# A two-layer trunk on one core: gate and up as 7 quarter products, down products between them, banded pooling

## Chip, core, metric

The kernel runs on one core of a Trainium2 chip. The metric is the device time of one execution in microseconds; the median of three runs before the change is 1806.95.

## What is computed

Tokens x (512 x 1024) pass two layers. Each layer has a SwiGLU feed-forward network (FFN) ahead of its mixer and one behind it, so there are four FFNs, each with its own weights and a root-mean-square norm of its input:

```python
def swiglu(u, wg, wu, wd):
    return (jax.nn.silu(u @ wg) * (u @ wu)) @ wd
...
h = h + 0.5 * swiglu(rmsnorm(h, ffn_pre_norm[l]), ffn_pre_wg[l], ffn_pre_wu[l], ffn_pre_wd[l])
u = rmsnorm(h, mix_norm[l])
```

wg and wu are 1024 x 2816, wd is 2816 x 1024. The mixer of the first layer is pooling: in four groups of 256 channels a causal mean over the last 2, 4, 8 or 16 tokens, less the token itself, times a 256 x 256 matrix. After the first layer the shared keys and values (kv) are made; the mixer of the second layer is latent attention over them. A final norm ends the program. All of it is float32.

## The kernel before

The residual lies transposed on the chip, as 8 tiles h0 to h7 of 128 channels x 512 tokens. Every product of float32 matrices is made as three products of rounded parts: each operand is split into a high part (ScalarE rounds it to fp32r) and a low part (VectorE subtracts), and `mm3` (L83 to L87) adds high x high, high x low and low x high in PSUM. `load_w` (L101) fetches 1024 columns of weights (512 KB) into one of four raw buffers, ScalarE casts them (L117), VectorE subtracts (L118).

`ffn` (L276) works on two halves of 11 blocks of 128 hidden features. For a block, 8 chunks x 3 matmuls of 512 tokens make gate, and as many make up. `gated` (L280) takes them out of PSUM: gate and up times the norm's factor (VectorE, L284 and L286), Silu (ScalarE), their product (GpSimd, L287), and the split of the product (ScalarE L290, VectorE L291). After 11 blocks come the 8 down products of that half, 33 matmuls each, added to h by VectorE (L324).

`Norm` (L209) follows each new h chunk: it multiplies by the gain and splits (`hi`, `lo`; L219, L224), squares it on ScalarE (L237) and adds the squares on GpSimd (L241). When all 8 chunks are there, TensorE sums over channels (L156), VectorE finds the reciprocal root with 12 small operations (`rsqrt`, L162), `on_all` (L193) builds a diagonal, multiplies it by ones on TensorE (L204) and ScalarE copies the result out (L206). The gate and up products use the unscaled h times the gain, so they don't wait for the norm's factor; only `gated` does.

In the pooling stage the products with the pooling matrices come first, and VectorE and GpSimd make the moving sums on 128 x 512 tiles by shifted additions (`shift`, L367 to L373); TensorE meanwhile runs products of the first blocks of the second FFN. At the very end the last two down products run in two halves of 256 tokens, and `first_half` (L719) norms and stores the first while the second is made. Before the fourth FFN stands the attention's output projection (`out_proj`, L531).

The order on each engine is that of a scheduler, except in the pooling stage, whose order on TensorE, VectorE and GpSimd is that of the code.

## Time and profile before

| what | us |
|---|---|
| three runs | 1803.35, 1806.95, 1807.29 |
| profiled execution: time, span of the records | 1802.47, 1800.7 |
| first FFN | 6.2 to 371.3 |
| pooling stage | 371.3 to 446.8 |
| second FFN | 446.8 to 773 |
| shared kv | 773 to 825 |
| third FFN | 825 to 1160 |
| attention | 1160 to 1428 |
| fourth FFN | 1428 to 1784.2 |
| last norm and store | to 1800.7 |

An execution's time is a little more than the span of its profile's records. The stages overlap by a few products; the limits are those of TensorE's work. Busy times count an engine's own instructions, and a matmul's duration in the records overlaps with the next one's: the pace is read from the distance of two starts.

### The profile page before, as it was taken

What the parts mean: (1) busy time and instruction counts of PE and PEld (TensorE: products, weight loads), DVE (VectorE), ACT (ScalarE), POOL (GpSimd) and SP (SyncE); (2) the same over time, 40 slices, a digit from 0 to 9 for tenths busy, and PEclk for the clock granted to TensorE, in tenths of its full rate; (3) what the DMA queues carried; (4) which work ended last, traced back from release to release, by engine and by line L of the source; (5) the groups of instructions that cost most, each with busy time, mean ns of one, the idle gap of its engine ahead of it and who ended that gap; (6) DMA issues with size and microseconds to landing.
All of it is one profiled execution on the core that took longest, in us unless ns stands there. A gap on an engine that the chain in (4) does not pass through costs nothing.

```text
span 1800.7 us, 20652 instructions
## 1 busy us (share of the span) xinstructions
PE 1757.8 (98%) x8120; PEld 1457.7 (81%) x8120; DVE 869.3 (48%) x1266; ACT 624.0 (35%) x940; POOL 340.0 (19%) x218
## 2 busy tenths in 40 slices
PE   8999999988999999999999999999999999999997
PEld 6888888866888888878888888888888888888886
DVE  7443444478443444456433443487665754334432
ACT  6322232323331233333322233277564432222221
POOL 3220022134220122102210122212121222101212
PEclk9999999989999999999999999999999999999998
DMA  7223223212222232223222322121231322322301
GB/s 258 94 94 103 96 94 96 104 59 70 92 96 94 96 103 94 94 87 107 94 94 99 100 94 76 59 71 51 74 94 59 129 94 96 103 94 94 101 29 47
DMA packets 49552, 165.77 MB, mean 92 GB/s; under 512 B 6448, under 2 KB 6448, under 8 KB 49456
## 3 DMA queue, kind: packets, MB, share of 16 engines
q1 hardware_dynamic: 49456, 164.46, 27.7%
q8 instruction: 64, 1.05, 0.2%
q14 instruction: 32, 0.26, 0.0%
HBM read 157.88 MB, written 2.10 MB: 89 GB/s over the span
## 4 chain that ended last, share of the span: by engine, by line
PE 93%; DVE 4%; issue 1%; ACT 1%; DMA 1%; SPq 0%; DVEq 0%; ACTq 0%
PE mm L85 30%; PE mm L86 29%; PE mm L87 29%; DVE s L372 1%; DVE wlo L118 1%; PE mm L615 1%; PE aux L156 1%; PE mm L614 1%; PE aux L651 1%; PE mm L626 0%; PE mm L616 0%; PE mm L627 0%; DVE gh_lo L224 0%; PE mm L651 0%; DVE h L381 0%
## 5 line engine op out<-in xcount | busy, mean ns | idle before, releaser
L85 PE MATMUL mm<-gh_hi,whi 128*128 128x512 f32 x1440 | 561.8, 393 | 15.8 <-ACT whi L117 6.2
L86 PE MATMUL mm<-gh_lo,whi 128*128 128x512 f32 x1440 | 565.0, 392 | 7.3 <-DVE gh_lo L224 7.3
L87 PE MATMUL mm<-gh_hi,wlo 128*128 128x512 f32 x1440 | 563.2, 392 | 0.0
L117 ACT CAST whi<-wraw 128x1024 fp32r<-128x1024 f32 (+2 forms) x332 | 315.2, 959 | 714.1 <-PE mm L86 647.1
L118 DVE TENSOR_TENSOR wlo<-wraw,whi 128x1024 fp32r<-128x1024 f32 (+2 forms) x302 | 372.4, 1235 | 195.6 <-ACT whi L117 195.1
L287 POOL TENSOR_TENSOR tu<-tu,tg 128x512 f32<-128x512 f32 x88 | 191.8, 2180 | 1014.7 <-ACT whi L117 762.7
L85 PEld LDWEIGHTS mm<-gh_hi,whi 128*128 128x128 f32 x1440 | 272.0, 189 | 76.3 <-ACT gh_hi L219 6.9
L86 PEld LDWEIGHTS mm<-gh_lo,whi 128*128 128x128 f32 x1440 | 272.6, 189 | 66.9 <-DVE gh_lo L224 9.8
L87 PEld LDWEIGHTS mm<-gh_hi,wlo 128*128 128x128 f32 x1440 | 272.5, 189 | 57.2 <-issue 0.2
L85 PE MATMUL mm<-mh,whi 128*128 128x512 f32 (+1 forms) x726 | 277.9, 383 | 0.0
L86 PE MATMUL mm<-ml,whi 128*128 128x512 f32 (+1 forms) x726 | 276.5, 383 | 0.0
L87 PE MATMUL mm<-mh,wlo 128*128 128x512 f32 (+1 forms) x726 | 276.4, 383 | 0.0
L286 DVE TENSOR_TENSOR tu<-mm,rb 128x512 f32<-128x512 f32 x88 | 60.8, 691 | 255.4 <-PE mm L87 255.4
L86 PEld LDWEIGHTS mm<-ml,whi 128*128 128x128 f32 x726 | 136.4, 188 | 26.7
L87 PEld LDWEIGHTS mm<-mh,wlo 128*128 128x128 f32 x726 | 136.4, 188 | 26.6
L85 PEld LDWEIGHTS mm<-mh,whi 128*128 128x128 f32 x726 | 136.4, 188 | 26.6
L291 DVE TENSOR_TENSOR ml<-tu,mh 128x512 fp32r<-128x512 f32 x88 | 62.7, 713 | 131.2 <-ACT mh L290 131.0
L290 ACT CAST mh<-tu 128x512 fp32r<-128x512 f32 x88 | 54.5, 621 | 188.0 <-POOL tu L287 187.2
L324 DVE SCALAR_TENSOR_TENSOR h<-mm,h 128x512 f32<-128x512 f32 (+1 forms) x66 | 44.5, 675 | 143.1 <-PE mm L87 143.0
L284 DVE TENSOR_TENSOR tg<-mm,rb 128x512 f32<-128x512 f32 x88 | 60.8, 691 | 80.7 <-PE mm L87 79.7
L241 POOL TENSOR_TENSOR sq_acc<-sq_acc,sq 128x512 f32<-128x512 f32 (+1 forms) x43 | 58.1, 1350 | 204.8 <-ACT sq L237 204.7
L118 POOL TENSOR_TENSOR wlo<-wraw,whi 128x512 fp32r<-128x512 f32 (+1 forms) x30 | 40.9, 1362 | 197.6 <-ACT whi L117 191.5
(158 smaller groups left out, 1424.8 us busy)
## 6 DMA issues: line engine op xcount, KB each, us to landing
wraw<-in_wgu SPq DMA_DIRECT2D x160, 512.0 KB, 3.3
wraw<-in_wd SPq DMA_DIRECT2D x88, 512.0 KB, 3.2
wraw<-in_wo SPq DMA_DIRECT2D x16, 512.0 KB, 3.3
wraw<-in_wfirst SPq DMA_DIRECT2D x12, 512.0 KB, 3.2
wraw<-in_wheads SPq DMA_DIRECT2D x8, 512.0 KB, 3.3
h<-in_xT SPq DMA_DIRECT2D x8, 256.0 KB, 5.6
wraw<-in_wfirst SPq DMA_DIRECT2D x8, 256.0 KB, 5.7
qr<-yh SPq DMA_DIRECT2D x32, 64.0 KB, 2.0
```

What stands on the lines that cost most here:

```text
L85: nc.tensor.matmul(out, w[0], x[0], start=start, stop=False)
L86: nc.tensor.matmul(out, w[0], x[1], start=False, stop=False)
L87: nc.tensor.matmul(out, w[1], x[0], start=False, stop=stop)
L117: nc.scalar.copy(hi[:, s], raw[:, s])
L118: lo_engines[i % len(lo_engines)].tensor_tensor(out=lo[:, s], in0=raw[:, s], in1=f(hi[:, s]), op=ALU.subtract)
L241: nc.gpsimd.tensor_tensor(out=self.acc[:, ts], in0=self.acc[:, ts], in1=self.sq[:, ts], op=ALU.add)
L284: nc.vector.tensor_tensor(out=tg, in0=gate, in1=rb, op=ALU.mult)
L286: nc.vector.tensor_tensor(out=tu, in0=up, in1=rb, op=ALU.mult)
L287: nc.gpsimd.tensor_tensor(out=tu, in0=tu, in1=tg, op=ALU.mult)
L290: nc.scalar.copy(hi, tu)
L291: nc.vector.tensor_tensor(out=lo, in0=tu, in1=f(hi), op=ALU.subtract)
L324: nc.vector.scalar_tensor_tensor(out=h[d][:, ts], in0=o[:, ts], scalar=0.5, in1=h[d][:, ts], op0=ALU.mult, op1=ALU.add)
```

## The change

Gate and up of one block g are x wg and x wu. Taken as one product of a matrix of quarters (channels 0 to 511 and 512 to 1023; the two outputs and the two token halves), they are made with 7 products instead of 8, by a form of Strassen's algorithm with 15 additions. Each product has 4 chunks of 128 channels x 3 matmuls x 256 tokens.

- Of the weights of a block, two 512 KB loads as before, four parts are split: gate's two quarters (`a`), one of up (`a22`), and the sums s1, s3 and s2, s4, whose four additions of 128 x 512 run on GpSimd (`group_weights`, L166). Before, the two loads alone were split. The raw buffers stay four, and the sums are made in place.
- Of h, `PairNorm` makes seven quarter operands per chunk pair (c, c + 4) in place of two halves: `row1` and `row2`, per pair 3 multiplications and 4 casts on ScalarE and 8 operations on VectorE.
- The outputs are put together by VectorE in PSUM and in small tiles (`p2`, `p7`, `p3`), in 7 operations of 256 tokens and one of 512 in place of two of 512; the product of gate and up moves from GpSimd to VectorE.
- The 22 blocks are in five parts (4, 4, 4, 4, 6). The down products of a part, two in each block, are laid behind the products of the next part's blocks, in PSUM tiles of another pool. Those of the last six blocks stand at the end. The order on TensorE is that of the code.
- Pooling: the pooling matrices' products are made with tokens on partitions, and the moving mean less the token is a product with a banded matrix of 128 x 144 (`pooled`), 9 matmuls a chunk. The shifted sums of VectorE and GpSimd, one to four a chunk, go.

```diff
+    def group_weights(raws, wb):
+        ra, rb = raws
+        q0, q1, whole = slice(0, 512), slice(512, UNIT), slice(0, UNIT)
+        def add(out, x, y):
+            nc.gpsimd.tensor_tensor(out=out, in0=x, in1=y, op=ALU.add)
+        a = split_w(ra, wsplit_sb, "w")
+        split_into(a, ra, whole)
+        a22 = split_w(rb[:, q0], room.wf, "f")
+        split_into(a22, rb[:, q0], q0)
+        add(rb[:, q0], rb[:, q0], rb[:, q1])
+        add(rb[:, q1], rb[:, q1], ra[:, q0])
+        s13 = split_w(rb, wsplit_sb, "w")
+        split_into(s13, rb, whole)
+        add(ra[:, q0], rb[:, q0], ra[:, q0])
+        add(ra[:, q1], ra[:, q0], ra[:, q1])
+        s24 = split_w(ra, wb, "w")
+        split_into(s24, ra, whole)
...
+        def row1(self, k):
+            b = self.b[k] = room.act.tile([P, 3, HT], F32, tag="g", name="b0", bufs=3)
+            nc.scalar.mul(b[:, ::2], h[k].rearrange("p (a b) -> p a b", a=2), gain(self.base, k))
+            nc.vector.tensor_tensor(out=b[:, 1], in0=b[:, 2], in1=b[:, 0], op=ALU.subtract)
+            ga = self.pair(resid, f"gh{k}")
+            self.split_pair(ga, b[:, :2].rearrange("p a b -> p (a b)"))
+            self.gh[k] = ga
+        def row2(self, k):
+            b = self.b.pop(k)
+            t1, b12 = b[:, 1], b[:, 2]
+            u = room.act.tile([P, 3, HT], F32, tag="g", name="b1", bufs=3)
+            c = k + ND // 2
+            b21, n22 = u[:, 0], u[:, 1]
+            nc.scalar.mul(b21, h[c][:, :HT], gain(self.base, c))
+            nc.scalar.mul(n22, h[c][:, HT:], g_neg[:, self.base + c:self.base + c + 1])
+            gb = self.pair(room.gx, f"gb{k}")
+            self.split_pair(gb, u[:, :2].rearrange("p a b -> p (a b)"))
+            t = room.act.tile([P, T], F32, tag="m", name="t24")
+            nc.vector.tensor_tensor(out=t[:, :HT], in0=t1, in1=n22, op=ALU.add)
+            nc.vector.scalar_tensor_tensor(
+                out=t[:, HT:], in0=t[:, :HT], scalar=-1.0, in1=b21, op0=ALU.mult, op1=ALU.subtract)
+            gc = self.pair(resid, f"gh{c}")
+            self.split_pair(gc, t)
+            t3 = room.act.tile([P, HT], F32, tag="c1", name="t3")
+            nc.vector.scalar_tensor_tensor(
+                out=t3, in0=n22, scalar=-1.0, in1=b12, op0=ALU.mult, op1=ALU.subtract)
+            if k % 2 == 0:
+                self.gd[k // 2] = self.pair(room.gx, f"gd{k // 2}")
+            self.split_pair(self.gd[k // 2], t3, slice(k % 2 * HT, (k % 2 + 1) * HT))
+            self.gh[c] = gb, gc
...
+            def product(g, to, w, x, ks=range(4), start=True, stop=True):
+                if start and ks[0] == 0:
+                    acc[g][to] = mm_tile()[:, :HT]
+                for k in ks:
+                    mm3(acc[g][to], weights[g][w](k), norm.operand(x, k), start and k == 0, stop and k == 3,
+                        skip_group_check=True)
...
+            def p1(g, ks=range(4)):
+                product(g, "x", "a11", "b11", ks)
+                if ks[-1] == 3:
+                    copy_of(g, "c1")
+            def p2(g, ks=range(4)):
+                product(g, "y2", "a12", "b21", ks)
+                if ks[-1] == 3:
+                    act[g]["g"] = room.act.tile([P, 3, HT], F32, tag="g", name="gate", bufs=3)
+                    y = acc[g]["y2"]
+                    nc.vector.tensor_tensor(out=y, in0=act[g].pop("c1"), in1=y, op=ALU.add)
+            def scaled(g, i, y):
+                nc.vector.tensor_tensor(
+                    out=act[g]["g"][:, i], in0=y, in1=factor["r"][:, i * HT:(i + 1) * HT], op=ALU.mult)
+            def p6(g):
+                product(g, "x", "s2", "n2", start=False)
+                copy_of(g, "c16")
+            def p5(g, ks=range(4)):
+                product(g, "y1", "s1", "t1", ks)
+            def p7(g):
+                product(g, "x", "s3", "t3", start=False)
+                t = copy_of(g, "c167")
+                nc.vector.tensor_tensor(out=t, in0=t, in1=acc[g]["y1"], op=ALU.subtract)
+            def p4(g):
+                product(g, "x", "a22", "t4", start=False)
+            def p3(g):
+                product(g, "y1", "s4", "n22", start=False)
+                y = acc[g].pop("y1")
+                nc.vector.tensor_tensor(out=y, in0=act[g]["c16"], in1=y, op=ALU.subtract)
+                scaled(g, 1, y)
+                gate = act[g]["g"][:, :2].rearrange("p a b -> p (a b)")
+                nc.scalar.activation(gate, gate, AF.Silu)
+                nc.vector.tensor_tensor(out=gate, in0=gate, in1=factor["r"], op=ALU.mult)
+                m = room.act.tile([P, T], F32, tag="m", name="m")
+                nc.vector.tensor_tensor(out=m[:, :HT], in0=acc[g].pop("x"), in1=gate[:, :HT], op=ALU.mult)
+                nc.vector.tensor_tensor(out=m[:, HT:], in0=act[g]["c167"], in1=gate[:, HT:], op=ALU.mult)
+                j = g % N_MID
                 hi = midp.tile([P, T], F32R, tag=f"mh{j}", name=f"mh{j}")
                 lo = midp.tile([P, T], F32R, tag=f"ml{j}", name=f"ml{j}")
...
+                nc.scalar.copy(hi, m)
+                nc.vector.tensor_tensor(out=lo, in0=m, in1=f(hi), op=ALU.subtract)
+                mids[g] = hi, lo
...
+            base, due, before = 0, [], None
+            for n in PARTS:
+                groups = list(range(base, base + n))
+                if base == 0:
+                    pair, groups = groups[:2], groups[2:]
+                    for g in pair:
+                        prepare(g)
+                    for k in range(3):
+                        for p in (p1, p5, p2):
+                            for g in pair:
+                                p(g, [k])
+                    for p in (p1, p5):
+                        for g in pair:
+                            p(g, [3])
+                    r = norm.r()
+                    for g in pair:
+                        p2(g, [3])
+                    p6(0)
+                    factor["r"] = norm.spread(r)
+                    for g in pair:
+                        scaled(g, 0, acc[g].pop("y2"))
+                    p6(1)
+                    p7(0)
+                    p7(1)
+                    p4(0)
+                    p3(0)
+                    before = 1
+                for g in groups:
+                    prepare(g)
+                    p1(g)
+                    p2(g)
+                    scaled(g, 0, acc[g].pop("y2"))
+                    p4(before)
+                    p6(g)
+                    p5(g)
+                    if g == NF - 1:
+                        p7(g)
+                        p3(before)
+                        p4(g)
+                        p3(g)
+                    else:
+                        p3(before)
+                        p7(g)
+                    before = g
+                    now, due = due[:2], due[2:]
+                    if len(due) == ND - 2:
+                        down_two(now, tile_of=aux_tile)
+                    else:
+                        for d in now:
+                            down(last_part, d, tile_of=aux_tile)
+                last_part, due = (base, n), list(ORDER)
+                base += n
...
+        def pooled(c):
+            g, cs, o = c // 2, slice(c * P, (c + 1) * P), mm_tile()
+            for tb in range(NQB):
+                n, table = min(BAND, T - tb * P), thi[:, g, int(tb == 0)]
+                os = o[:, tb * P:tb * P + n]
+                nc.tensor.matmul(os, vh[:, tb, cs], table[:, :n], start=tb == 0, stop=False, skip_group_check=True)
+                nc.tensor.matmul(os, vl[:, tb, cs], table[:, :n], start=False, stop=tb == NQB - 1,
+                                 skip_group_check=True)
+                if tb == 0:
+                    nc.tensor.matmul(o[:, :PAD], vh[:, tb, cs], tlo[:, g], start=False, stop=False,
+                                     skip_group_check=True)
             nc.vector.scalar_tensor_tensor(
...
+                out=h[c], in0=o, scalar=gain(G_PSCALE, c), in1=h[c], op0=ALU.mult, op1=ALU.add)
+            nxt.add(c)
+        with tc.manual_schedule(engines={mybir.EngineType.PE}):
+            os = {(0, tb): product(0, tb) for tb in range(NQB)}
             r = rms(norm.squares, D)
...
+            for tb in range(2):
+                os[1, tb] = product(1, tb)
+            for tb in range(NQB):
+                values_of(0, tb, os[0, tb])
+            for tb in range(2, NQB):
+                os[1, tb] = product(1, tb)
+            for tb in range(NQB):
+                values_of(1, tb, os[1, tb])
+            for c in ORDER:
```

**VectorE, start of the first FFN.** Before (gh_lo and wlo are the low parts of the x chunk and of the weights):

```order
L224 SCALAR_TENSOR_TENSOR gh0_lo_162<-h0_82,g_sb_90,gh0_hi_161 128x512
L118 TENSOR_TENSOR wlo_100<-wraw_98,whi_99 128x512
L224 SCALAR_TENSOR_TENSOR gh1_lo_168<-h1_83,g_sb_90,gh1_hi_167 128x512
L118 TENSOR_TENSOR wlo_100<-wraw_98,whi_99 128x512
L224 SCALAR_TENSOR_TENSOR gh2_lo_175<-h2_84,g_sb_90,gh2_hi_174 128x512
L118 TENSOR_TENSOR wlo_111<-wraw_109,whi_110 128x512
```

Each x chunk (of h_82, h_83, h_84) was followed by the piece of weights that goes with it. With the change (gb, gd, gh are low parts of x quarters with 0 to 3 the chunk, wraw_107 and wraw_109 the second loads of blocks 0 and 1, wraw_106 and wraw_108 the first):

```order
L354 TENSOR_TENSOR gb2_lo_218<-b1_214,gb2_hi_217 128x512
L354 TENSOR_TENSOR gd1_lo_231<-t3_228,gd1_hi_230 128x256
L375 TENSOR_TENSOR t24_256<-b0_237,b1_249 128x256
L381 SCALAR_TENSOR_TENSOR t3_263<-b1_249,b0_237 128x256
L354 TENSOR_TENSOR gh6_lo_225<-t24_221,gh6_hi_224 128x512
L354 TENSOR_TENSOR gh3_lo_241<-b0_237,gh3_hi_240 128x512
L376 SCALAR_TENSOR_TENSOR t24_256<-t24_256,b1_249 128x256
L157 TENSOR_TENSOR wlo_293<-wraw_106,whi_292 128x1024
L354 TENSOR_TENSOR gb3_lo_253<-b1_249,gb3_hi_252 128x512
L157 TENSOR_TENSOR wlo_307<-wraw_109,whi_306 128x1024
L354 TENSOR_TENSOR gd1_lo_231<-t3_263,gd1_hi_230 128x256
L354 TENSOR_TENSOR gh7_lo_260<-t24_256,gh7_hi_259 128x512
```

Now the operands of chunks 2 and 3 stand ahead of the last weight sums of both blocks.

**TensorE, start of the first FFN**, with the change, from the second item on (mm_320 and mm_328 are sums of block 1, whi_306 and wlo_307 its s1 and s3):

```order
L91 MATMUL mm_320<-gh0_hi_144,whi_296 128x256
L92 MATMUL mm_320<-gh0_lo_145,whi_296 128x256
L93 MATMUL mm_320<-gh0_hi_144,wlo_297 128x256
L91 MATMUL mm_324<-gh0_hi_144,whi_286 128x256
L92 MATMUL mm_324<-gh0_lo_145,whi_286 128x256
L93 MATMUL mm_324<-gh0_hi_144,wlo_287 128x256
L91 MATMUL mm_328<-gh0_hi_144,whi_306 128x256
L92 MATMUL mm_328<-gh0_lo_145,whi_306 128x256
L93 MATMUL mm_328<-gh0_hi_144,wlo_307 128x256
L91 MATMUL mm_332<-gb0_hi_153,whi_276 128x256
L92 MATMUL mm_332<-gb0_lo_154,whi_276 128x256
```

Before, four sums took one chunk after the other, high parts first. Now p1, p5 and p2 of both blocks take chunk 0, and p5 of block 1 comes fourth.

**TensorE, the last down products.** Before, inside the second token half (mm_13205):

```order
L86 MATMUL mm_13205<-ml8_12632,whi_13092 128x256
L87 MATMUL mm_13205<-mh8_12631,wlo_13093 128x256
L156 MATMUL aux_13163<-ones_157,sq_13159 128x1
L156 MATMUL aux_13163<-ones_157,sq_acc_12826 128x1
L156 MATMUL aux_13163<-ones_157,sq_13159 128x1
L85 MATMUL mm_13205<-mh9_12703,whi_13092 128x256
L86 MATMUL mm_13205<-ml9_12704,whi_13092 128x256
L87 MATMUL mm_13205<-mh9_12703,wlo_13093 128x256
L85 MATMUL mm_13205<-mh10_12775,whi_13092 128x256
L86 MATMUL mm_13205<-ml10_12776,whi_13092 128x256
```

The product that spreads the norm (L204) came after all of them. With the change, between the first token half (mm_18979) and the second (mm_19045):

```order
L91 MATMUL mm_18979<-mh5_18765,whi_18962 128x256
L92 MATMUL mm_18979<-ml5_18766,whi_18962 128x256
L93 MATMUL mm_18979<-mh5_18765,wlo_18963 128x256
L236 MATMUL aux_19003<-ones_138,sq_acc_18817 128x1
L236 MATMUL aux_19003<-ones_138,sq_18999 128x1
L236 MATMUL aux_19003<-ones_138,sq_acc_18817 128x1
L236 MATMUL aux_19003<-ones_138,sq_18999 128x1
L284 MATMUL aux_19025<-diag_19023,ones_138 128x256
L91 MATMUL mm_19045<-mh0_18085,whi_18925 128x256
L92 MATMUL mm_19045<-ml0_18086,whi_18925 128x256
L93 MATMUL mm_19045<-mh0_18085,wlo_18926 128x256
```

The token sums of the first half and the product that spreads its norm now stand together ahead of them.

## Rows read from the trace of the kernel before

**Rows 1.** The page, part 1: busy time, share of the span and instructions of each engine.

```profile
PE 1757.8 (98%) x8120; PEld 1457.7 (81%) x8120; DVE 869.3 (48%) x1266; ACT 624.0 (35%) x940; POOL 340.0 (19%) x218
```

**Rows 2.** Windows by stage: length, busy (x instructions) of PE, PEld, DVE, ACT, POOL; PEclk, DMA.

```profile
6.24:40.00 33.76, 33.62 (x141) 27.14 (x142) 29.50 (x40) 21.19 (x31) 8.64 (x7) 1.00 0.82 283
40.00:371.30 331.30, 331.30 (x1463) 274.32 (x1462) 136.51 (x147) 97.94 (x119) 56.45 (x28) 1.00 0.29 98
371.30:446.80 75.50, 58.63 (x230) 43.78 (x228) 64.64 (x83) 20.58 (x28) 34.79 (x32) 0.89 0.15 50
...
773.00:825.00 52.00, 50.58 (x232) 41.48 (x231) 33.07 (x59) 19.76 (x25) 3.84 (x2) 1.00 0.27 87
...
1428.00:1784.20 356.20, 356.20 (x1643) 297.64 (x1643) 137.36 (x170) 97.83 (x120) 56.33 (x29) 1.00 0.25 82
```

**Rows 3.** PE timeline, N=512 products: start, duration; 1759.77 to 1765.89 is 27 intervals.

```profile
1759.77 0.39 PE L87 MATMUL mm<-mh,wlo 128*128 128x512 f32 x1
...
1765.89 0.39 PE L87 MATMUL mm<-mh,wlo 128*128 128x512 f32 x1
```

**Rows 4.** PE timeline, N=256 products: 1767.48 to 1775.63 is 68 intervals.

```profile
1767.48 0.28 PE L85 MATMUL mm<-mh,whi 128*128 128x256 f32 x1
...
1775.63 0.28 PE L87 MATMUL mm<-mh,wlo 128*128 128x256 f32 x1
```

**Rows 5.** PE timeline, the first N=512 products.

```profile
6.24 0.79 PE L85 MATMUL mm<-gh_hi,whi 128*128 128x512 f32 x1 [6.24 <-ACT whi L117]
...
7.25 0.63 PE L85 MATMUL mm<-gh_hi,whi 128*128 128x512 f32 x1
7.68 0.63 PE L86 MATMUL mm<-gh_lo,whi 128*128 128x512 f32 x1
...
11.88 0.39 PE L86 MATMUL mm<-gh_lo,whi 128*128 128x512 f32 x1
```

**Rows 6.** DVE timeline at the start: start, duration, operation.

```profile
5.19 0.75 DVE L224 SCALAR_TENSOR_TENSOR gh_lo<-h,g_sb,gh_hi 128x512 fp32r<-128x512 f32 x1 [4.16 <-ACT gh_hi L219]
...
13.72 1.78 DVE L118 TENSOR_TENSOR wlo<-wraw,whi 128x512 fp32r<-128x512 f32 x1
15.43 1.78 DVE L224 SCALAR_TENSOR_TENSOR gh_lo<-h,g_sb,gh_hi 128x512 fp32r<-128x512 f32 x1
...
19.50 0.68 DVE L118 TENSOR_TENSOR wlo<-wraw,whi 128x512 fp32r<-128x512 f32 x1
20.11 0.74 DVE L224 SCALAR_TENSOR_TENSOR gh_lo<-h,g_sb,gh_hi 128x512 fp32r<-128x512 f32 x1
```

**Rows 7.** POOL timeline, the same stretch and after.

```profile
39.63 1.30 POOL L287 TENSOR_TENSOR tu<-tu,tg 128x512 f32<-128x512 f32 x1 [21.27 <-ACT tg L285]
...
100.37 2.37 POOL L287 TENSOR_TENSOR tu<-tu,tg 128x512 f32<-128x512 f32 x1 [8.51 <-ACT whi L117]
```

**Rows 8.** DVE timeline in a middle loop.

```profile
100.36 1.23 DVE L118 TENSOR_TENSOR wlo<-wraw,whi 128x1024 fp32r<-128x1024 f32 x1 [0.17 <-ACT whi L117]
```

**Rows 9.** Groups by form on DVE: busy us, mean ns, idle before.

```profile
L286 DVE TENSOR_TENSOR tu<-mm,rb 128x512 f32<-128x512 f32 x88 | 60.8, 691 | 255.4 <-PE mm L87 255.4
L234 DVE TENSOR_TENSOR sq<-h 128x256 f32<-128x256 f32 x2 | 0.9, 426 | 0.2
```

**Rows 10.** Groups by form on ACT.

```profile
L117 ACT CAST whi<-wraw 128x1024 fp32r<-128x1024 f32 x264 | 277.9, 1053 | 684.6 <-PE mm L86 627.4 <-issue 44.4 <-DMA wraw<-in_wgu 8.5
```

**Rows 11.** DVE timeline, the norm before the pooling.

```profile
375.90 0.16 DVE L182 TENSOR_SCALAR mean<-aux 128x4 f32<-128x4 f32 x1 [1.11 <-PE aux L156]
...
378.35 0.69 DVE L197 TENSOR_TENSOR diag<-ident,rms_r 128x512 f32<-128x512 f32 x1
381.63 1.41 DVE L361 SCALAR_TENSOR_TENSOR v<-mm,g_sb,rb 128x512 f32<-128x512 f32 x2 [2.59 <-ACT rb L206]
```

**Rows 12.** Timeline of all engines at the end, the first token half's norm.

```profile
1779.61 0.16 DVE L182 TENSOR_SCALAR mean<-aux 128x2 f32<-128x2 f32 x1 [3.07 <-PE aux L156]
...
1782.84 0.43 DVE L197 TENSOR_TENSOR diag<-ident,rms_r 128x256 f32<-128x256 f32 x1
```

More of the change, by code (lines that the diff above doesn't have):

```diff
@@ new lines, in trunk_kernel, with split_w, split_into, raw_tiles @@
+    room = Room()
+    room.open()
+    def split_w(raw, pool, tag, lo_engine=None):
+        n = raw.shape[-1]
+        hi = pool.tile([P, n], F32R, tag=f"{tag}hi", name=f"{tag}hi")
+        lo = pool.tile([P, n], F32R, tag=f"{tag}lo", name=f"{tag}lo")
+        return hi, lo
+    def split_into(tiles, raw, s):
+        hi, lo = tiles
+        nc.scalar.copy(hi[:, s], raw[:, s])
+        nc.vector.tensor_tensor(out=lo[:, s], in0=raw[:, s], in1=f(hi[:, s]), op=ALU.subtract)
+    def raw_tiles():
+        return [wraw_sb.tile([P, UNIT], F32, tag="wraw", name="wraw") for _ in range(2)]
@@ new lines, in trunk_kernel, with first_load, load_x @@
+    first_raws = [raw_tiles() for _ in range(2)]
+    def first_load(i, k, s):
+        nc.sync.dma_start(first_raws[i][k][:, s], wgu[0, i, k, :, s])
+    def load_x(c):
+        nc.sync.dma_start(h[c], xT[:, c])
+    q0, q1 = slice(0, 512), slice(512, UNIT)
+    load_x(0)
+    first_load(0, 0, q0)
+    load_x(4)
+    first_load(0, 0, q1)
+    first_load(1, 0, slice(0, UNIT))
+    load_x(1)
+    load_x(5)
+    first_load(0, 1, slice(0, UNIT))
+    load_x(2)
+    load_x(6)
+    first_load(1, 1, slice(0, UNIT))
@@ L338, in trunk_kernel, with down @@
-    norm = Norm(G_PRE)
-    for c in range(ND):
+                nc.scalar.copy(hi, m)
+                nc.vector.tensor_tensor(out=lo, in0=m, in1=f(hi), op=ALU.subtract)
+                mids[g] = hi, lo
+                del weights[g], act[g]
+            blocks, units, o_of, seen = {}, {}, {}, [0]
+            whole = slice(0, T)
+            def down(part_of, d, ts=whole, js=None, tile_of=mm_tile):
+                base, n = part_of
+                js = js or range(n)
+                o = o_of.pop((d, ts.start), None) or tile_of()
+                for j in js:
+                    key = d, base + j
+                    if key not in blocks:
+                        blocks[key] = seen[0]
+                        seen[0] += 1
+                    u, k = divmod(blocks[key], 8)
+                    if u not in units:
+                        units[u] = part(load_w(wd[idx, u]), 8, P)
+                    mm3(o[:, ts], [x[:, k] for x in units[u]], [x[:, ts] for x in mids[base + j]], j == 0, j == n - 1)
+                if js[-1] != n - 1:
+                    o_of[d, ts.start] = o
+                    return
+                nc.vector.scalar_tensor_tensor(
+                    out=h[d][:, ts], in0=o[:, ts], scalar=-0.5, in1=h[d][:, ts], op0=ALU.mult, op1=ALU.add)
+                if base + n == NF:
+                    on_h(d, ts)
@@ new lines, in down_two @@
+            def down_two(ds, **kw):
+                n = last_part[1]
+                for js in (range(n - 1), [n - 1]):
+                    for d in ds:
+                        down(last_part, d, js=js, **kw)
+            base, due, before = 0, [], None
[50 more added lines that the diff above has]
+                base += n
@@ L340, in trunk_kernel @@
+            down_two(ORDER[:2])
+            n_whole = ND - 2 if last else ND
+            for d in ORDER[2:n_whole]:
+                down(last_part, d)
+            for th in range(2):
+                for d in ORDER[n_whole:]:
+                    down(last_part, d, slice(th * HT, (th + 1) * HT))
+    norm = PairNorm(G_PRE)
+    for c in ORDER:
         norm.add(c)
     nc.sync.dma_start(rope_sb, rope)
-    nc.sync.dma_start(wfix_sb, wfix)
     nxt = Norm(G_MIX)
-    ffn(0, norm, nxt.add, first=first_w)
@@ L481, in __init__, with r, spread @@
             mean = mean_of(token_sums(norm.squares), D)
-            self.gh, self.r = norm.gh, on_all(rsqrt(mean, "rms_r"))
-            shared_kv(mean, self.r)
-        def rb(self):
-            return self.r
+            self.operand, self.rb = norm.operand, on_all(rsqrt(mean, "rms_r"))
+            shared_kv(mean, self.rb)
+        def r(self):
+            return None
+        def spread(self, r):
+            return self.rb
     nxt = Norm(G_MIX + ND)
     ffn(2, Shared(norm), nxt.add)
-    more.clear()
     room.close()
-    norm, nxt = nxt, Norm(G_POST + ND)
+    norm, nxt = nxt, PairNorm(G_POST + ND)
     with tc.tile_pool(name="att", bufs=2) as ap_, tc.tile_pool(name="att1", bufs=1) as a1:
```

298 lines of the change are left out of this document (129 added, 169 removed).

## Prediction

> **What bounds the kernel now.** I read first the busy times of the engines, then the windows by stage, then the timelines of single engines for prices. TensorE is busy for 1757.8 of 1800.7 us [rows 1], so the kernel is bound by the number of matmuls times their pace. The windows show where it is not [rows 2]: 16.9 us of the 75.5 us pooling stage are idle on TensorE, while VectorE is busy for 64.6 of them; elsewhere almost nothing is. Inside an FFN (40 to 371 us) TensorE has no idle time and VectorE works 136.5 of 331.3 us. So matmul time removed inside an FFN comes off the end, as long as VectorE and GpSimd keep feeding; and whatever the change adds for these two at the four starts of an FFN meets a TensorE that has nothing else to do there.
>
> The profiled execution took 1802.5 us, 4.5 us under the median of the three runs (1806.95) and 0.9 under the fastest. The sum is made against 1802.5. A difference of 0.2% (3.6 us) is about what a measurement of this kernel can tell from none.
>
> **Products.** An N=512 matmul starts every (1765.89 - 1759.77)/27 = 0.2267 us [rows 3], an N=256 one every (1775.63 - 1767.48)/68 = 0.120 us [rows 4]. A block of 128 hidden features needed 2 x 8 x 3 = 48 of the first kind, 10.88 us; it now needs 7 x 4 x 3 = 84 of the second, 10.08 us. 0.80 us less for 88 blocks is **-70 us** (17.6 per FFN). Seven eighths of the columns would be 1.36 us less, but half the columns take 0.53 of the time. The down products keep their number and width. [...] The 68 intervals stand in one unbroken run of the same three-product form, so I take 0.80.
>
> **The prices of the preparation.** The first products start at 6.24 us and run at an interval of 0.43 us until about 11.5 [rows 5]: half pace after an idle stretch. VectorE's first operation is at 5.19; one of 512 columns then takes 0.61 us of its time (19.50 to 20.11), but 1.71 us (13.72 to 15.43) while GpSimd adds squares [rows 6]. A GpSimd operation of 512 columns takes 1.30 us alone, and 2.37 us when a VectorE weight subtraction starts with it [rows 7]; that is 1.23 us long itself [rows 8]. So the two take turns when both operands lie in SBUF: a GpSimd operation costs a busy VectorE 1.1 us in the one pair of rows and 1.07 in the other; with some overlap I take 1.05, between nothing (rival 1) and its whole 1.30 (9 us more in all). VectorE operations with an operand in PSUM stay at 0.69 us in the mean of 88; a 256-column one takes 0.43, 0.40 without the overlap [rows 9]. A cast of 1024 columns on ScalarE takes 1.05 us [rows 10].
>
> **Start of the first FFN.** In the order of the changed kernel the fourth piece on TensorE (three matmuls; four such pieces make one of the seven products) needs wlo_307, the lower part of the second block's s1/s3. That is the 38th of VectorE's operations on x and weights: 14 of 512 columns (8.5 us), 19 of 256 (7.6), 5 of 1024 (5.7, at 1.14), 21.8 us. Twelve GpSimd operations lie ahead of it (6 square sums, 6 weight additions): 12.6 us of turns. From 5.2 us that gives 40 us. Then 21 pieces of 0.36 us, and some 2.5 us at half pace: 50. Before, products ran from 6.24 us on with every chunk as it landed.
>
> What follows hangs together as a chain. The norm needs its token sums (51 us); from the mean to a spread result took 5.7 us before (375.90 to 381.63) [rows 11], less the copy after the matmul, but here a 1024-column and two 256-column operations stand between: the spreading matmul comes at 56. TensorE has only p2's last piece and p6(0) ahead of it, and p6(1) stands behind it. p6(1), p7(0), p7(1) end at 61; only then can VectorE do two subtractions and block 2's a22 (62.5), which two GpSimd additions wait for (65), then a cast, two more additions (68), a cast and a subtraction (70). TensorE had work until 68; the rest of blocks 2 and 3 at 1.44 us a product, with one more such wait of about 1, ends p7(3) at **86 us**. Without waits it would be 6.2 + 26 x 1.44 = 43.7. Of the 42 us before's own FFN lost 6 (365.1 us against 1584 x 0.2267 = 359.1 [rows 2, 3]): **+36 us**.
>
> **Pooling and second FFN.** Before, three blocks' products were done when the 75.5 us stage ended, four would have been at 86.4 us. Now: r on tokens at 10 us (two weight subtractions stand ahead of the mean), then 28 VectorE operations of 512 (17.4), 18 of 256 (7.2), 3 of 1024 (3.4), 9 GpSimd turns (9.5) and some 2 us until the first pooled product: 50 us. The shifted sums are gone and the banded products cost TensorE only 72 x 0.12 = 8.6 us, in its idle time. Then the same chain, 1.4 + 36 us, ends p7(3) at 88. Two products are owed (2.9) and 3.2 us counted in the -70 are missed here: 88 + 2.9 + 3.2 - 86.4 = 8; ScalarE's casts, which alternate with VectorE's subtractions, may add 5. I take **+10**.
>
> **Third and fourth FFN.** The kv stage loses 1.4 us on TensorE now and the fourth FFN none [rows 2]. Between the kv products and the gate products the spread of the kv norm is waited for (4 us, as in rows 11 with less ahead), then block 2's weights (4.5: the same chain of additions and casts, with no norm's wait ahead of it to hide a part) and block 4's (2): **+10**. Before the fourth FFN the x rows are 26.6 us on VectorE with 13 GpSimd turns (13.6), 40 us; TensorE has the last two output-projection chunks (96 x 0.2267 = 21.8) and 24 pieces (8.6), so it waits 10, and the chain costs 6 more, as in the first FFN (50 to 86 is 36 us for 20.5 products of 1.44, 29.5): **+16**.
>
> **The very end.** Before, the first half's token sums lay among the second half's products, and its norm (mean at 1779.61, diagonal done at 1783.27) was hidden [rows 12]. Now the sums and the spreading matmul stand together ahead of all the second half's products: 0.9 us for the residual and squares, 3.7 for the norm, about 1.4 around: **+6**.
>
> **The loops.** With two down products a loop is 10.08 + 24 x 0.2267 = 15.52 us on TensorE. VectorE has four operations of 1024 columns (4.6), five of 512 (3.1) and seven of 256 (2.8) there, and four GpSimd turns (4.2), 14.7 in all: hidden, with 0.8 us in hand. Blocks 20 and 21 have no down products beside them; 10.08 us faces some 12: about 2.3 us an FFN, **+9**. Small slips, 0.1 us in 64 loops: **+6**. Weight loads are two of 512 KB a block as before, at a DMA share of 0.29 [rows 2].
>
> **Sum.** -70 + 36 + 10 + 10 + 16 + 6 + 9 + 6 = +23; 1802.5 + 23 = 1825.5, said as **1826 us**. The starts carry about 15 us either way, the slips 6 down and 6 up: 1805 to 1845 for this case.
>
> **Rivals.**
> 1. *The turns cost nothing at the starts* (faster). VectorE waits there for casts and loads anyway, and GpSimd's additions fall into these waits. For it: in the first window of 33.8 us VectorE was busy 29.5, not all. Against it: the stretched rows follow each other without a gap [rows 6]. 12 + 9 + 3 + 13 = 37 turns of 1.05 are 39 us: 1826 - 39 = **1787**. It decides the sign when more than 22 of the 37 turns are free.
> 2. *The loops become bound by the weights' chain* (slower still). The chain of a block goes through VectorE, GpSimd, ScalarE, GpSimd, ScalarE, VectorE, and 0.8 us in hand is little. A loop of 16.0 in place of 15.52 and my 0.1 is 0.4 x 64 = 26 us: **1852**. It decides from 15.6 us a loop on.
> 3. *Half the columns take half the time* (faster). The 0.120 us of rows 4 would be a matter of that place, and 84 matmuls at 0.1133 take 9.52 us: 0.56 us x 88 = 49 us more off, **1777**. The rows show one pace over 68 intervals, in a stage with a granted clock of 1.00 [rows 2], so it gets little. [...]
>
> **How the numbers follow.** Forecast 0.56, rival 1 0.22, rival 2 0.13, rival 3 0.07, something else 0.02. Faster by over 0.2%: rivals 1 and 3 and 0.03 of the forecast's low end, 0.32. Slower: the rest but 0.04 for no difference, 0.64. The range reaches from between rivals 1 and 3 (1780) to the upper half of rival 2 (1860).
>
> **What would show it.** N=256 products should start every 0.12 us in unbroken runs. TensorE should be nearly idle between about 7 and 40 us, waiting for wlo_307's subtraction, and p7(3) should end near 86. A loop with down products should last 15.5 to 15.7 us. A p7(3) that ends before 62 us, or loops over 16, would make the prediction wrong.

## The result, and the profile after

The changed kernel takes 1930.05 us (median of 4 runs, 1927.75 to 1936.22) against 1806.65 us in the same sessions: a ratio of 1.0692, 95% interval 1.0664 to 1.0721. It is slower, as forecast, but by 123 us instead of 19, and outside the range. The head of the page and its part 1 answer to [rows 1]:

```profile
span 1929.4 us, 28759 instructions
...
PE 1751.2 (91%) x11376; PEld 1599.4 (83%) x11376; DVE 1351.0 (70%) x2141; ACT 888.9 (46%) x1464; POOL 656.0 (34%) x456
```

TensorE's idle time grew from 42.9 to 178.2 us. Its busy time fell by 6.6 us only, and not by the 70 us that the smaller number of products saves, among other things because some of them ran at half pace (0.21 us an interval instead of 0.120, below). The waits of TensorE, summed by what ended them (us in total, times, longest):

```profile
PE mm L93 <- DVE wlo L157: 65.2, 18, 10.4
PE mm L91 <- ACT whi L156: 31.0, 6, 11.6
PE aux L91 <- ACT mh L499: 20.6, 16, 1.8
PE aux L284 <- DVE diag L277: 16.9, 5, 7.8
PE mm L91 <- ACT kvh_hi L405: 9.6, 1, 9.6
PE mm L92 <- DVE gh_lo L354: 8.9, 4, 5.5
PE aux L92 <- DVE ml L500: 7.9, 16, 0.6
```

96 us are waits for split weights (L156, L157), 9.35 of them at the very start of the program; 28.5 us, in 32 waits, are for the product of gate and up of the block just finished (its high and low part, mh and ml; "mids" below). The windows by stage answer to [rows 2] (length, busy of PE, PEld, DVE, ACT and POOL with their counts, then the granted clock, DMA share and GB/s):

```profile
9.35:96.40 87.05, 49.39 (x330) 46.61 (x331) 61.62 (x86) 37.69 (x64) 36.23 (x26) 0.94 0.24 78
96.40:418.90 322.50, 310.01 (x2066) 285.58 (x2065) 229.10 (x315) 140.43 (x204) 115.76 (x77) 0.99 0.31 99
418.90:502.70 83.80, 65.44 (x432) 62.75 (x431) 66.62 (x108) 42.38 (x72) 30.86 (x21) 0.80 0.16 50
...
835.30:912.60 77.30, 51.71 (x283) 45.34 (x282) 51.65 (x86) 30.75 (x48) 22.41 (x16) 0.76 0.15 45
...
1525.00:1602.50 77.50, 58.73 (x410) 56.54 (x411) 53.13 (x86) 31.80 (x51) 28.47 (x19) 0.81 0.20 66
```

The four starts are where TensorE idles, and the granted clock there is 0.76 to 0.94 in the mean. But the long stretch 96 to 419 us, all loops and end products, idles 12.5 us too, where [rows 2] has nothing. By the start of the last down product's last matmul the FFNs end at 418.9, 835.3, 1248.0 and 1918.5 us; before at 371.1, 773.1, 1149.2 and 1784.1. So the first FFN lost 47.8 us, pooling and the second 14.4, kv and the third 36.6, the rest 29.9.

**The loops themselves are as forecast.** Two starts of p1 in neighbouring loops without a wait:

```profile
313.62 0.28 PE L91 MATMUL mm<-gh_hi,whi 128*128 128x256 f32 x1
...
329.16 0.28 PE L91 MATMUL mm<-gh_hi,whi 128*128 128x256 f32 x1
```

15.54 us, against 15.52. The products cost what [rows 4] say, 0.120 us each, so the 0.80 us a block of [rows 3, 4] were saved, and half the columns in half the time, 0.1133 us (rival 3), is out.

**The start of the first FFN.** TensorE's waits of the first 45 us, and VectorE in the same time:

```profile
23.39 0.58 PE L91 MATMUL mm<-gh_hi,whi 128*128 128x256 f32 x1 [11.57 <-ACT whi L156]
34.60 0.58 PE L93 MATMUL mm<-gh_hi,wlo 128*128 128x256 f32 x1 [10.42 <-DVE wlo L157]
42.77 0.58 PE L93 MATMUL mm<-gh_hi,wlo 128*128 128x256 f32 x1 [6.52 <-DVE wlo L157]
```

```profile
18.95 1.75 DVE L354 TENSOR_TENSOR gb_lo<-b,gb_hi 128x512 fp32r<-128x512 f32 x1
...
27.39 1.48 DVE L381 SCALAR_TENSOR_TENSOR t<-b,b 128x256 f32<-128x256 f32 x1
28.79 1.48 DVE L376 SCALAR_TENSOR_TENSOR t<-t,b 128x256 f32<-128x256 f32 x1
30.19 1.48 DVE L359 TENSOR_TENSOR b<-b 128x256 f32<-128x256 f32 x1
...
38.23 0.68 DVE L354 TENSOR_TENSOR gh_lo<-t,gh_hi 128x512 fp32r<-128x512 f32 x1
...
41.50 1.21 DVE L157 TENSOR_TENSOR wlo<-wraw,whi 128x1024 fp32r<-128x1024 f32 x1
```

The fourth piece ran at 42.77 us; 40 was forecast. Operations of 256 columns take 1.48 us here and 0.41 alone, those of 512 columns 1.75 and 0.68 (38.23 and its like are undisturbed): 1.07 us for each turn, the same for both sizes. Between 5 and 41.5 us GpSimd does 14 operations, 6 square sums and 8 additions, and just 14 VectorE operations are stretched so, by 14.9 us in all.

**Block 2.** ScalarE, VectorE, GpSimd and TensorE from 67 to 80 us, one fence each as the timelines give them:

```profile
67.14 0.62 ACT L156 CAST fhi<-wraw 128x512 fp32r<-128x512 f32 x1 [0.95 <-PE mm L92]
...
74.39 1.04 ACT L156 CAST whi<-wraw 128x1024 fp32r<-128x1024 f32 x1
```

```profile
67.80 0.69 DVE L157 TENSOR_TENSOR flo<-wraw,fhi 128x512 fp32r<-128x512 f32 x1 [1.14 <-ACT fhi L156]
...
73.94 2.64 DVE L157 TENSOR_TENSOR wlo<-wraw,whi 128x1024 fp32r<-128x1024 f32 x2
76.50 0.68 DVE L500 TENSOR_TENSOR ml<-m,mh 128x512 fp32r<-128x512 f32 x1
77.10 0.68 DVE L157 TENSOR_TENSOR flo<-wraw,fhi 128x512 fp32r<-128x512 f32 x1
77.71 1.21 DVE L157 TENSOR_TENSOR wlo<-wraw,whi 128x1024 fp32r<-128x1024 f32 x1
```

```profile
68.57 5.79 POOL L170 TENSOR_TENSOR wraw<-wraw 128x512 f32<-128x512 f32 x4 [30.88 <-DVE flo L157]
```

```profile
75.49 0.39 PE L91 MATMUL mm<-gh_hi,whi 128*128 128x256 f32 x1 [2.51 <-ACT whi L156]
75.71 0.28 PE L92 MATMUL mm<-gh_lo,whi 128*128 128x256 f32 x1
78.97 0.58 PE L93 MATMUL mm<-gh_hi,wlo 128*128 128x256 f32 x1 [2.98 <-DVE wlo L157]
79.35 0.42 PE L91 MATMUL mm<-gh_hi,whi 128*128 128x256 f32 x1
```

The cast of a22 is released by TensorE: it needs one of the two buffers of a22 (pool wf), which p4(0) frees at 67.1. Most of that lateness lies ahead of it: the spreading matmul started at 58.77 us instead of 56, the products behind it ran at half pace until 62.3 (granted clock 0.50 from 59.6 on), and so p7(1) ended at 65.6 instead of 61. By the release that the prediction named, VectorE's two subtractions behind p7(1), a22 could have gone on at 66.65; the buffer put its subtraction at 67.80, 1.2 us later. Then four additions one after the other until 74.4, a cast, and the subtraction, which stands behind three other operations in VectorE's queue: 10.4 us from a22 to the last weights instead of 7.5. p6(2) runs on at 78.97, not 70. The two waits, 2.51 and 2.98 us, come in all four FFNs, and others of 2.65 to 2.69 at block 4, whose weights are made ready beside block 3, and at block 21; blocks 0 to 3, 20 and 21 have no down products beside them. After the second wait the products run at an interval of 0.21 us until 83 us, at a granted clock of 0.51 between 79.4 and 83.0, 1.00 again from 84 on.

**The first down product of a part.** It needs the mids of the block just finished. VectorE, ScalarE and TensorE at the second such place of the first FFN, where p3, the last product that the mids need, has just ended:

```profile
174.18 0.43 DVE L488 TENSOR_TENSOR mm<-c,mm 128x256 f32<-128x256 f32 x1 [3.10 <-PE mm L93]
...
174.98 1.31 DVE L157 TENSOR_TENSOR wlo<-wraw,whi 128x1024 fp32r<-128x1024 f32 x1
176.21 1.78 DVE L492 TENSOR_TENSOR gate<-gate,rb 128x512 f32<-128x512 f32 x1
177.92 1.21 DVE L123 TENSOR_TENSOR wlo<-wraw,whi 128x1024 fp32r<-128x1024 f32 x1
```

```profile
180.16 0.62 ACT L499 CAST mh<-m 128x512 fp32r<-128x512 f32 x1 [1.62 <-DVE m L495]
```

```profile
180.83 0.49 PE L91 MATMUL aux<-mh,whi 128*128 128x512 f32 x1 [1.15 <-ACT mh L499]
```

From 174.18 to the end of the cast it takes 6.6 us, with two weight subtractions (L157, L123) and a turn in L492 (1.78 us instead of 0.68) on the way. TensorE has one product and 18 down matmuls for that time, 5.5 us. The way takes 6.6 us at 12 of the 16 such places and 7.0 to 7.2 at the other four.

### The profile page after: what moved, and what is told of

It is laid out like the page before. It is cut to its first block, busy times and chain, and to the rows that moved or that the text cites. A ratio compares the mean times of both kernels' runs of the same rounds, so it can differ in the third digit from the quotient of the medians.

```text
span 1929.4 us, 28759 instructions
## 1 busy us (share of the span) xinstructions
PE 1751.2 (91%) x11376; PEld 1599.4 (83%) x11376; DVE 1351.0 (70%) x2141; ACT 888.9 (46%) x1464; POOL 656.0 (34%) x456
## 3 DMA queue, kind: packets, MB, share of 16 engines
q8 instruction: 89, 1.46, 0.3%
## 5 line engine op out<-in xcount | busy, mean ns | idle before, releaser
L170 POOL TENSOR_TENSOR wraw<-wraw 128x512 f32<-128x512 f32 x352 | 532.2, 1512 | 889.9 <-DVE flo L157 839.5
L156 ACT CAST whi<-wraw 128x1024 fp32r<-128x1024 f32 x264 | 276.3, 1050 | 281.5 <-POOL wraw L170 219.3
L93 PE MATMUL mm<-gh_hi,wlo 128*128 128x256 f32 (+1 forms) x1072 | 319.3, 298 | 65.2 <-DVE wlo L157 65.2
L157 DVE TENSOR_TENSOR wlo<-wraw,whi 128x1024 fp32r<-128x1024 f32 x264 | 337.9, 1282 | 25.8 <-ACT whi L156 25.8
L91 PE MATMUL mm<-gh_hi,whi 128*128 128x256 f32 (+1 forms) x1072 | 320.0, 298 | 31.3 <-ACT whi L156 31.0
L92 PE MATMUL mm<-gh_lo,whi 128*128 128x256 f32 (+1 forms) x1072 | 316.9, 296 | 8.9 <-DVE gh_lo L354 8.9
L92 PEld LDWEIGHTS mm<-gh_lo,whi 128*128 128x128 f32 x1072 | 217.9, 203 | 14.7 <-DVE gh_lo L354 9.9
L91 PE MATMUL aux<-mh,whi 128*128 128x512 f32 x512 | 202.8, 396 | 20.6 <-ACT mh L499 20.6
L92 PE MATMUL aux<-ml,whi 128*128 128x512 f32 x512 | 203.7, 398 | 7.9 <-DVE ml L500 7.9
L91 PE MATMUL mm<-gb_hi,whi 128*128 128x256 f32 x704 | 201.9, 287 | 1.5 <-DVE kvt L688 1.5
L488 DVE TENSOR_TENSOR mm<-c,mm 128x256 f32<-128x256 f32 x88 | 37.7, 428 | 217.6 <-PE mm L93 217.6
L123 DVE TENSOR_TENSOR wlo<-wraw,whi 128x1024 fp32r<-128x1024 f32 (+2 forms) x122 | 149.8, 1228 | 31.6 <-ACT whi L122 31.3
```

The source lines that it names most:

```text
L91: nc.tensor.matmul(out, w[0], x[0], start=start, stop=False, **kw)
L92: nc.tensor.matmul(out, w[0], x[1], start=False, stop=False, **kw)
L93: nc.tensor.matmul(out, w[1], x[0], start=False, stop=stop, **kw)
L123: lo_engines[i % len(lo_engines)].tensor_tensor(out=lo[:, s], in0=raw[:, s], in1=f(hi[:, s]), op=ALU.subtract)
L156: nc.scalar.copy(hi[:, s], raw[:, s])
L157: nc.vector.tensor_tensor(out=lo[:, s], in0=raw[:, s], in1=f(hi[:, s]), op=ALU.subtract)
```

## The experiments

Two theories stood against each other: the additions of the weights (their chain through three engines, and GpSimd's turns with VectorE) cost the time, or the operands made from h and the order of products do.

**The mids earlier.**

```diff
                     p4(before)
+                    p3(before)
                     p6(g)
                     p5(g)
+                    p7(g)
                     if g == NF - 1:
-                        p7(g)
-                        p3(before)
...
```

> Edit: p3 of the block before is issued directly behind p4, ahead of p6 and p5 of the running block. Theory A (at the first loop of each part TensorE waits 1.1 to 1.8 us for mh and 0.2 to 0.6 for ml of the block just finished, because p3 stands two products behind p4): the mids are ready 2.9 us earlier, the 32 waits (28.5 us in all) and the half-pace matmuls behind them go: about 1895 us. Theory B (the weights' chain sets these places, the mids only show last): the wait moves to the lower parts of the weights, no change, 1925 to 1935 us.

Measured 1880.07 us, 50 us less (ratio to before 1.0416, 1.0393 to 1.0438). Theory A, and 15 us more than it said: the waits for mh are gone, those for ml fell from 7.9 to 3.0 us, and the matmul groups on wlo wait 10 times instead of 18 (45.2 us): the waits at blocks 4 and 21 are gone, where p6, the first reader of s2, now stands one product later. In exchange there are 19 us of new waits for c tiles, at blocks 2, 4 and 21. So the 50 us are more than the mids alone.

**No additions.**

```diff
         def add(out, x, y):
-            nc.gpsimd.tensor_tensor(out=out, in0=x, in1=y, op=ALU.add)
+            pass
```

> Edit: the four weight additions of a block on GpSimd are left out, so s1 to s4 are plain quarters and the output is not the reference's; all casts, subtractions and products stay. Theory A (the chain subtraction, two additions, cast, two additions, cast, subtraction, and GpSimd's turns with VectorE, set the starts and the blocks without down products): wlo of the second block lands near 34 us instead of 42.8, the 5.5 us at block 2 and 2.7 us at blocks 4 and 21 of each FFN go or shrink to under 1: about 1850 us. Theory B (the operands made from h on VectorE set the starts): the starts keep their length, under 30 us off: 1900 us or more.

Measured 1811.89 us: 118 of the 123 us (9.6 of them the wait for kvh_hi, of which the next run tells). Theory A, and more than it said. TensorE's largest waits there:

```profile
PE aux L284 <- DVE diag L277: 19.3, 5, 7.1
PE mm L91 <- ACT whi L156: 17.8, 3, 9.1
PE mm L93 <- DVE wlo L157: 12.0, 6, 3.8
```

The waits for L156 and L157 fall from 96 to 30 us, the fourth piece of the first FFN runs at 26.1 us instead of 42.8, and the first three FFNs end at 381.8, 772.5 and 1154.7. L492 takes 0.68 us in all 88 blocks, and the way from p3 to the mids 5.2 to 5.3 us at the 16 places above, under the 5.5 us that TensorE has for it: the waits for mh are gone too.

**The additions on VectorE.**

```diff
-            nc.gpsimd.tensor_tensor(out=out, in0=x, in1=y, op=ALU.add)
+            nc.vector.tensor_tensor(out=out, in0=x, in1=y, op=ALU.add)
```

> Edit: the four weight additions run on VectorE instead of GpSimd. Theory A (an addition costs a busy VectorE about 1.05 us of turn on GpSimd and only 0.61 us on itself, and two handovers go): the first FFN's start is 2 to 4 us earlier, block 2's weights 3 to 4 us, so 25 to 35 us off: about 1900 us. Theory B (VectorE is the bound of the loops once it carries 2.4 us more): loops of 16 us or more, slower than 1930.

Measured 1885.42 us (1.0445, 1.0425 to 1.0465), 45 us less: Theory A, in sign and somewhat over its size. The fourth piece ran at 37.96 us. The kv stage no longer waits 9.6 us for kvh_hi. In the changed kernel ScalarE does these two casts behind a cast of PairNorm (L353), which waits for a stretched VectorE operation (L359, 1.48 us instead of 0.42); here it does them ahead of it. That order is the scheduler's and not the code's (only TensorE's is): the two casts stand behind in the three kernels with the additions in the chain on GpSimd, and ahead in the other runs of the changed kernel. So a run compares two kernels each with its own order on the other engines; no run held that order fixed.

**The additions behind the splits**, first on GpSimd, then on VectorE (the same edit and L170 changed as above):

```diff
         split_into(a22, rb[:, q0], q0)
+        s13 = split_w(rb, wsplit_sb, "w")
+        split_into(s13, rb, whole)
+        s24 = split_w(ra, wb, "w")
+        split_into(s24, ra, whole)
         add(rb[:, q0], rb[:, q0], rb[:, q1])
         add(rb[:, q1], rb[:, q1], ra[:, q0])
-        s13 = split_w(rb, wsplit_sb, "w")
-        split_into(s13, rb, whole)
         add(ra[:, q0], rb[:, q0], ra[:, q0])
         add(ra[:, q1], ra[:, q0], ra[:, q1])
-        s24 = split_w(ra, wb, "w")
-        split_into(s24, ra, whole)
```

> Edit: the four additions of a block stay on GpSimd, but behind all four splits, so that nothing but the next load waits for them; s1 to s4 are plain quarters and the output is not the reference's. With no additions at all it was 1812 us, with them in the chain 1930. Theory A (the handovers of the chain cost the time: the casts and subtractions of s wait for GpSimd): near 1812, under 1830 us. Theory B (the turns cost it: a GpSimd addition holds up VectorE wherever it runs): 1860 us or more.

> Edit: the four additions of a block behind all four splits, as in the run with 1889 us, but on VectorE; s1 to s4 are plain quarters and the output is not the reference's. The raw buffers come free as late as there. Theory A (the 77 us over the kernel without additions were the turns of GpSimd with VectorE): four operations of 0.61 us on VectorE itself are cheaper than four turns of 1.05, 60% of the 77 or less: 1840 to 1858 us. Theory B (the late raw buffers and loads cost them): about 1889 us again.

Measured 1889.31 and 1849.13 us. With the others they make a table:

| additions | none | behind the splits | in the chain |
|---|---|---|---|
| on GpSimd | 1811.9 | 1889.3 | 1930.1 |
| on VectorE | 1811.9 | 1849.1 | 1885.4 |

Read along a row: work that no product waits for costs 77 us on GpSimd and 37 on VectorE; putting it into the chain costs 41 and 36 more (of the 41, 9.6 are the wait for kvh_hi). So the larger half is the time that the additions take from VectorE, by turns or by running on it. In both kernels of the middle column the DMA queue waits for the additions about as long before it may load again (1142 and 1172 us in all), so late loads don't make the 40 us between them: these are what the turns cost more than the same additions on VectorE. Whether the 37 us are VectorE's time alone or late loads in part was not tried apart. TensorE's largest waits with the additions behind the splits on GpSimd:

```profile
PE aux L91 <- ACT mh L499: 35.7, 16, 4.0
PE aux L284 <- DVE diag L277: 21.0, 5, 8.5
PE mm L91 <- ACT whi L156: 18.3, 3, 9.0
PE mm L93 <- DVE wlo L157: 17.0, 6, 5.3
```

The weights are nearly in time again (as with no additions), but the mids are later than in the changed kernel: the way from p3 to mh takes 7.1 us at 12 places and 8.5 at four (before the move 6.6 and 7.0 to 7.2), with turns in L123 and L495 (at the first of the four 2.28 us instead of 1.21, and 1.15 instead of 0.41).

**Both edits, and the order of the first pair.**

> Edit: p3 of the block before directly behind p4, and the four weight additions on VectorE, together. Theory A (joints of the parts and weights' chain are two separate losses): the gains add, 1930 - 50 - 45 = about 1835 us. Theory B (both remove the same waits, or VectorE with the additions delays the mids): 1850 us or more.

Measured 1858.68 us (1.0290, 1.0249 to 1.0332): Theory B. The gains don't add, 71 us of 95: with the additions on VectorE the subtraction of ml comes later, and its waits are 9.8 us.

```diff
                     p6(0)
+                    p7(0)
+                    p6(1)
+                    p4(0)
+                    p7(1)
                     factor["r"] = norm.spread(r)
                     for g in pair:
                         scaled(g, 0, acc[g].pop("y2"))
-                    p6(1)
-                    p7(0)
-                    p7(1)
-                    p4(0)
                     p3(0)
```

> Edit: additions on VectorE; p3 of the block before directly behind p4 where the loop before had down products; and in the first pair the order p6(0), p7(0), p6(1), p4(0), p7(1), spread of the norm, p3(0), so that no product stands behind the spread's wait and a22's buffer of block 0 comes free 4 us earlier. Theory A: the 2.5 to 3 us waits for the diagonal go in three FFNs with the half pace behind them, and block 2's weights come 3 to 4 us earlier in all four: 20 to 28 us under the kernel with both edits, about 1812 us if that is 1835. Theory B (block 2's weights wait for VectorE, not for the buffer): only the diagonal's part, 8 to 12 us under.

> Edit: the same two changes of order as in the run before, with the additions on GpSimd. Theory A: the order's gains hold without the move of the additions: 1930 - 50 - 20 = about 1860 us. Theory B (with GpSimd in the chain the weights stay late whatever the order): 1880 us, as with p3 alone.

Measured 1837.56 and 1884.73 us. Both runs make two changes: the order of the first pair, and p3 moved only in loops 5 to 20 (at blocks 2 to 4 and 21 it stays where the changed kernel has it). With the additions on VectorE they are worth the 21 us of Theory A against the run with both edits; TensorE's waits for the diagonal fall from 19.5 to 8.7 us. With GpSimd they are worth 45 us against the changed kernel, 5 less than p3 alone (Theory B). In the trace of the second, p7(1) and p4(0) no longer stand behind the spread's wait, and block 2 waits 0.68 and 1.57 us instead of 2.51 and 2.98 (the first FFN, TensorE's waits):

```profile
69.10 0.39 PE L91 MATMUL mm<-gh_hi,whi 128*128 128x256 f32 x1 [0.68 <-ACT whi L156]
71.18 0.58 PE L93 MATMUL mm<-gh_hi,wlo 128*128 128x256 f32 x1 [1.57 <-DVE wlo L157]
```

In the second and fourth FFN these waits shrink likewise; in the third, which has no spread at that place, they stay (2.35 and 2.65). That points to the spread's wait more than to the buffer. A third buffer for a22 alone was not tried.

**The order without additions.**

> Edit: the two changes of order, and no weight additions at all (s1 to s4 are plain quarters, the output is not the reference's): what would be left if the additions were free. Theory A (without the additions the joints and block 2 no longer wait, so the order matters only for the norm's spread in three FFNs): 8 to 15 us under the 1812 us without additions, about 1800. Theory B (the order is worth as much as with additions on GpSimd, 45 us): about 1770 us.

Measured 1797.42 us (0.9949, 0.9929 to 0.9970): Theory A. This is what the change would give in that order if the additions were free: 0.5% under the kernel before, of which the pooling, next, is more than all.

**The pooling alone**, in the kernel before: `shift`, `scaled` and `finish` replaced by `pooled` as in the change, FFNs untouched.

> Edit: the kernel before with the banded pooling alone, FFNs as before. Theory A (the pooling stage is bound by VectorE's and GpSimd's shifted sums, 16.9 us of TensorE idle): the stage loses its shifts, TensorE gets 8.6 us of banded products: 8 to 14 us off, about 1795 us. Theory B (norm chains bound the stage): 1803 to 1810 us.

Measured 1790.41 us, ratio 0.9915, interval 0.9900 to 0.9930: Theory A at its upper end, faster than both kernels, and the fastest of all ten. Of the waits of the kernel before, those for gh_lo and gh_hi are the pooling stage's; the 6.2 us for whi are the program's start. First before, then the pooling alone:

```profile
PE mm L86 <- DVE gh_lo L224: 7.3, 5, 2.3
PE mm L85 <- ACT whi L117: 6.2, 1, 6.2
PE mm L85 <- ACT gh_hi L219: 6.1, 2, 4.1
```

```profile
PE mm L86 <- ACT whi L118: 6.3, 1, 6.3
PE mm L86 <- ACT pth L263: 2.3, 2, 1.8
PE mm L86 <- DVE pvl L267: 1.6, 1, 1.6
```

The 13.4 us for gh_lo and gh_hi are gone; of the new lines only the 1.6 us for pvl, the pooled operand, belong to the stage.

This run is the one to compare the FFNs with. Without additions the changed kernel still takes 21 us more (1811.89 against 1790.41), although its FFNs save 70 us of products: some 90 us of costs stay that the additions don't explain. So the other theory holds for a part. TensorE's waits without additions are 80 us against 29 in the kernel before; what these costs are, beyond such waits, was not tried run by run.

## Why the prediction was wrong

The step that failed is "The loops": VectorE's work there, turns and all, was held to be hidden because its sum was shorter than a loop, and so the additions had a price at the starts only (37 turns, 39 us, and the chains). By the run without them they cost 118 us. The direction was forecast, the size was not.

- **Products, -70 us: right.** 15.54 us a loop against 15.52.
- **Start of the first FFN: right to the fourth piece, 10 us short behind it.** 42.8 us against 40 and token sums at 52.1 against 51; the price of 1.05 us a turn held (1.07), and there were 14 turns instead of 12. One of the two pairs of rows behind that price was misread: in [rows 7, 8] it is GpSimd's operation that is stretched by VectorE's (2.37 us instead of 1.30). Behind the token sums the spread came at 58.8 instead of 56, with half pace after its wait; the buffer of a22 cost 1.2 us more, which "only then can VectorE do two subtractions and block 2's a22 (62.5)" doesn't have; and the chain from a22 took 10.4 us instead of 7.5, its last subtraction waiting for its place in VectorE's queue. p7(3) ended at 96.4, not 86.
- **"The loops ... hidden, with 0.8 us in hand": wrong.** The sum of VectorE's work per loop was compared with the loop, and a sum says nothing of when one result is due. The sum itself was too high: VectorE is busy for 10.3 and 11.4 us of two loops of 15.54, not 14.7. But at the first down product of a part the mids of the block just finished are needed 5.5 us after p3, and the way from p3 to mh took 6.6 to 7.2, with weight subtractions between its steps in VectorE's queue and, at 12 of 16 places, a turn in L492: 32 waits, 28.5 us. Not one of them is in the sum; its 6 us for slips was the only cover. Moving p3 took 50 us off, these waits and others; leaving out the additions brought the way down to 5.2 to 5.3 us.
- **Blocks 20 and 21, +9: right. Block 4: missed.** At block 21 TensorE waits 2.66 us in each FFN, 10.6 in all. The same wait at block 4, 2.68 us in each, is in the sum for the third FFN only (2 us).
- **Kv, 4 us of the +10: too small.** Waits of 9.64, 1.19, 7.81 and 1.46 us. The first stood in no term: kvh_hi was late behind a cast that waited for VectorE's stretched steps (1.74 and 1.48 us instead of 0.68 and 0.42), in an order of ScalarE that the runs without that wait don't have.
- **Half pace, put in once with 2.5 us: too small.** Intervals over 1.25 times those of [rows 3, 4], without a wait, add up to some 21 us above them in the trace before and to 51 after. 2.68 us of idle time at 103.81 was followed by 0.21 us an interval for about 3 us. TensorE was idle for 178.2 us instead of 42.9, and the half pace cost some 30 us more.
- **The very end, +6: not found.** The wait was there (0.91 and 2.95 us, with sums and spread 5.6), but from the last down matmul to the end it took 10.9 us instead of 16.6.
- **Rivals.** Rival 1 (turns free at the starts) is refuted by the 14 stretched operations there. Rival 2 had the right kind of mechanism in the wrong place: the loops as such are bound by TensorE (15.54 us); what waits is the first down product of a part, for its mids, and blocks 2, 4 and 21, for their weights.

That the time taken from VectorE is the larger half and the chain the smaller is shown by the table; how the 77 us divide among starts, first down products and kv was only read from waits. The exact share of the half pace was not tried alone.

## What to carry to other kernels

Compare a result's latency with the time until it is first needed, at each place where the cover changes (the first of a part, blocks without the interleaved work, the last): a sum of busy time per loop under the loop's length is no proof of cover. When an operand waits, look for the buffer that it is written into and the last reader of that buffer's old contents, besides its inputs. An arithmetic saving paid for with additions on a second engine that shares turns with the first (here 1.07 us for each) has to be priced with those turns at every place where the first is late; here 70 us of matmuls were bought with additions that cost 118, and with some 90 us more that stay without them.

## What the runs showed of the hardware

At the start of the first FFN each of the 14 VectorE operations with all operands in SBUF that began while a GpSimd operation of 512 columns with SBUF operands ran took 1.07 us longer, whether it had 256 columns (0.41 to 1.48) or 512 (0.68 to 1.75): 2.6 times its own time at 256 columns, 1.6 times at 512. The delay was a little under the 1.30 us that a GpSimd operation took alone [rows 7].

The VectorE operations of L465 and L488, with one input in PSUM, were not delayed: 82 of the 176 of L465 and 76 of the 88 of L488 ran while GpSimd worked, and every one kept its 0.41 to 0.43 us. L492, with both inputs in SBUF, took 0.7 us in the 24 blocks where GpSimd was idle and 1.5 to 1.8 in the 64 where it worked.

An addition of 512 columns that no product waits for cost 77/352 = 0.22 us of the total on GpSimd and 0.11 on VectorE itself.

Of TensorE's 13 waits of 2.65 to 2.98 us in the changed kernel, nine were followed by products at half pace (granted clock 0.50). After 2.68 to 2.69 us at block 4 the granted clock was 0.50 for about 3 us in all four FFNs; after 2.65 to 2.66 us at block 21 it was 1.00 in all four. In the first FFN TensorE had waited 2.98 us at 78.97, 25 us before the wait of block 4; before that of block 21 (377.69) it had run without a wait since 312.4.
